# One encoder block on one core: the low-rank gate product one unit sooner, both gate transposes ahead of one half unit, and one 7-product unit fewer in the mixer's output product

## The chip, the cores and the metric

The kernel runs on one core of one Trainium2 chip. Five engines work side by side, each with its own queue of instructions: PE multiplies matrices into PSUM, DVE and ACT do elementwise work, POOL a little of it, SP issues DMAs. The metric is the device time of one run in microseconds (us), the median of the runs shown.

## The reference

All data is float32; 256 frames of width 2048. One layer does, in this order: half a SwiGLU, the mixer, cross-attention to 256 memory tokens, half a SwiGLU. The change lies in the mixer, the third line on:

```python
def reference(x, mem, ...):
    x = x + 0.5 * swiglu(rms_norm(x, ffn1_norm[l]), ...)
    h = rms_norm(x, mix_norm[l])
    proj = h @ w_in[l]
    u, q, k, v, g, a_lr = jnp.split(proj, list(IN_SPLITS), axis=-1)     # a_lr: 16 columns
    y_pool = pool_mixer(u, pool_w[l], pool_scale[l])
    y_gla = gla_mixer(q, k, v, g, a_lr, gla_w_a2[l], gla_b_a[l], gla_head_norm[l])
    x = x + jnp.concatenate([y_pool, y_gla], axis=-1) @ w_out[l]
    x = x + mem_cross_attention(rms_norm(x, xattn_norm[l]), rms_norm(mem, mem_norm[l]), ...)
    x = x + 0.5 * swiglu(rms_norm(x, ffn2_norm[l]), ...)
    return rms_norm(x, final_norm)

def gla_mixer(q, k, v, g, a_lr, w_a2, b_a, head_norm):
    log_a = jax.nn.log_sigmoid((a_lr @ w_a2 + b_a)) / GLA_GATE_TEMP     # decay of every channel
    ...  # cumulative decays within chunks of 64 frames scale q and k; chunk-causal attention -> o
    o = o * lax.rsqrt(jnp.mean(o * o, axis=-1, keepdims=True) + RMS_EPS)
    return (o * head_norm) * jax.nn.silu(g)
```

## The kernel before, in words

**Numbers.** A float32 operand is split in two parts of type fp32r: a high part (ACT's cast, `wh` for weights) and a low part (DVE's difference, `wl`). A product is three matmuls: high by high, high by low, low by high. A matmul has a moving side of 128x512.

**Units.** All weights come through one stream of units of 1 MB: 256 rows of the weight by 1024 columns. Three loads are ahead (tile `raw`, three buffers), two splits are ahead (`wh`, `wl`, three buffers). A *plain* unit (`unit_p`, its matmuls recorded at L362) takes 24 matmuls. A *7-product* unit (`unit_s` and `seven`, recorded at L507) saves one product in eight and takes 21, but needs sums: of the activations, made once by `Sums.make` (DVE at L424 to L436, ACT and DVE at L285 and L286), and of the weights, made by `split_seven` for each unit (tile `T`: DVE at L486; then ACT at L279 and L489, DVE at L280 (`xl`) and L453).

**Blocks.** `block_s` takes eight units (2048 rows) for 1024 output columns. Its `order` says in which order the eight row pairs are taken, its `sevens` which of them are 7-product units, `amid` what else is put between two of them. The plain sums live in two PSUM tiles, the extra products of the 7-product units in two more; there are four PSUM tiles in all. `combine` (L581 to L586) and `join` (L596) merge them. `behind={n: (j, f)}` makes the matmuls of half `j` of the block's n-th unit stand behind the instruction that `f` gives, in PE's queue.

**The mixer.** `w_in` is taken in four blocks: q and k, pooling, v, gates. After the first stands the low-rank unit: `load_a` (L1056), `split_a` (L1065 and two parts), `a_unit` (16 matmuls into `pa`, L1072), `ev_a` (the tile `aT`, L1081 to L1083). `decay_logits` (L1088, tile `pz`) multiplies it with `gla_w_a2` ahead of the second half of the pooling block's first unit; ACT works on it (L1094 to L1102) and `decay` takes it up on DVE (scans at L1107, then L1114). `ev_g` and `gate` finish the gates: PE turns them in two groups of eight transposes (`rows_turned`, tile `ph`, L789), group 1 before group 0, and DVE multiplies (L1253) and splits the result into the activations `ys` of the output product. That is `into_x` with the plan `MIXED`: two blocks of eight units of `w_out`, whose result is added to `x` (L779, L767); `fold` turns `x` (tile `px`, L800) and splits it into `xs` (L248, L240) for the cross-attention, whose queries (`w_q`) follow.

**Order.** The code emits work unit by unit (`Stream`): `st.op(f, n)` puts `f` behind the next n units. Within what the dependences and `in_turn`, `behind_weights` and `issue_after` allow, the framework's scheduler sets the order on each engine. The homes of a tile in memory are shared: `T` and some `xh` of the output product lie in the two buffers `kv`, which the two 1 MB halves of `mem` take over (L1325).

Of the kernel before, what the change touches and what calls it, by code (L numbers as in the profile page):

```python
# [20 lines left out]
NB = 512  # L21
# [78 lines left out]
def build(ctx, tc, I, out):  # L100
    nc = tc.nc
    st = Stream()
# [87 lines left out]
    xs = main.tile([P, KT, 2, S], F32R, tag="xs", name="xs")  # L190
# [74 lines left out]
    def behind_weights(f):  # L265

        with tc.issue_after(latest["vector"].ins), tc.issue_after(latest["scalar"].ins):
            return f()
# [366 lines left out]
    def wload(dst, w, k0, n, n0, cols=NB):  # L635
        nc.sync.dma_start(
            dst, w[k0 * P : (k0 + n) * P, n0 : n0 + cols].rearrange("(k p) n -> p k n", p=P)
        )
# [9 lines left out]
    def wwide(w, n0, k0=0, nk=KT):  # L648

        def src(k):  # L650
            def load(raw):
                raw = raw.rearrange("p (k n) -> p k n", n=2 * NB)
                if len(loaded) < 3:
                    for kk in range(2):
                        parts = (0, NB) if not loaded else (0,)
                        for c in parts:
                            n = 2 * NB // len(parts)
                            wload(raw[:, kk : kk + 1, c : c + n], w, k + kk, 1, n0 + c, n)
                else:
                    wload(raw, w, k, 2, n0, 2 * NB)  # L660
                next(first_loads, None)
                loaded.append(1)
            return load
        return [src(k0 + k) for k in range(0, nk, 2)]
# [146 lines left out]
    class IntoX:  # L811
# [7 lines left out]
        def make_sums(self, after=None):  # L819
            for g, n in zip(self.sums.pairs, after or self.after):  # L820
# [1 line left out]

    WHOLE = IntoX((0, 4), (2, 5), ((1, 2, 3, 5, 0, 6, 4, 7), (1, 2, 0, 3, 4, 5, 6, 7)),
                  ((0, 4), (0, 4)))
    MIXED = IntoX((0, 4, 6), (1, 4, 9), ((1, 2, 3, 6, 0, 5, 4, 7), (1, 2, 0, 3, 4, 5, 6, 7)),
                  ((0, 4), (0, 4, 6)), room=3, folds=(1, 1, 2, 2))
    OUTPUT = IntoX((0, 4, 6), (0, 4, 9), ((1, 2, 3, 5, 0, 6, 4, 7), (1, 2, 0, 3, 4, 5, 6, 7)),
                   ((0, 4), (0, 4, 6)), room=3, folds=(1, 1, 2, 2))
    REST = IntoX((0,), (2,), ((1, 2, 3, 4, 0, 5), None), ((0,), ()), False)
# [2 lines left out]
    def into_x(w, act, scale, gain=None, k0=0, nk=KT, spread_too=True, src=None, way=OUTPUT,  # L832
               spread_at=3, behind=None):

        for b in range(2):
            st.op(lambda b=b: fetch_x(b, src), 2)
            cols = wwide(w, b * 2 * NB, k0, nk)
            if way.sevens[b]:
                block_s(cols, act, way.sums, way.orders[b], residual(scale, b, 0),
                        early_parts(scale, b), way.sevens[b], behind=None if b else behind)  # L840
            else:
                block_t(cols, act, residual(scale, b))
            if gain is not None:
                for j in range(2):
                    st.op(lambda c=2 * b + j: fold(c, gain), way.folds[2 * b + j])
        if gain is not None:
            st.op(lambda: finish_norm(4, spread_too), way.folds[3] + 1)
            if spread_too:
                st.op(spread_norm, spread_at)
# [94 lines left out]
    def in_ys(i):  # L944
        t = ys[:, 2 * i : 2 * i + 2].rearrange("p k a s -> p (k a s)")
        return t.rearrange("p (a n s) -> p a n s", a=2, n=4)

    qk_sums = Sums("qe", xs, (1, 3), False, 2, {0: in_ys(6), 1: in_ys(7)})
# [16 lines left out]
    w_in = I["w_in"][0]  # L965
    mix = {}
# [172 lines left out]
    def turn_qk(j):  # L1139
        if "kq" not in mix:  # L1140
            mt("kq", [P, 4 * LINES])
        t = mix["k" if j else "q"] = mix["kq"][:, j * H * S : (j + 1) * H * S].rearrange(
            "p (h s) -> p h s", h=H
        )
        nc.scalar.copy(t, rows_turned(mix["rows", j]))
# [29 lines left out]
    def queries(h):  # L1175
        q, E, F = mix["q"][:, h, :], mix["E"], mix["F"]
        e = lambda c: E[:, 4 * h + c : 4 * h + c + 1]
        f = lambda i: F[:, i, h : h + 1]
        QD = mix["QD", h] = m4()
        at = QD_AT  # L1180
        factors = {(0, 1): e(1), (0, 2): f(0), (0, 3): f(2), (1, 2): e(2), (1, 3): f(1), (2, 3): e(3)}
        for j in range(3):
            nc.scalar.copy(QD[:, at[j] + j * CH : at[j] + (j + 1) * CH], q[:, j * CH : (j + 1) * CH])
            for c in range(j + 1, 4):
                nc.vector.tensor_scalar_mul(
                    QD[:, at[j] + c * CH : at[j] + (c + 1) * CH], q[:, c * CH : (c + 1) * CH],
                    factors[j, c],
                )

    def scores(h):  # L1190
        q, kd, QD, at = mix["q"][:, h, :], mix["k"][:, h, :], mix["QD", h], QD_AT
        ps = ptile(uid("pq"))
        for j in range(4):
            part = slice((j % 2) * CH, (j % 2 + 1) * CH)
            rhs = QD[:, at[j] + j * CH : at[j] + S] if j < 3 else q[:, 3 * CH :]
            nc.tensor.matmul(
                ps[part, j // 2, j * CH : S], kd[:, j * CH : (j + 1) * CH], rhs, start=True, stop=True
            )
        s = score_tile(h)
        for j in range(4):  # L1200
            part = slice((j % 2) * CH, (j % 2 + 1) * CH)
            nc.scalar.copy(s[part, j // 2, j * CH :], ps[part, j // 2, j * CH : S])
# [56 lines left out]

    ORDER_IN = (0, 2, 4, 1, 5, 3, 6, 7)  # L1260
    st.op(query_rows, 3)
    block_s(wwide(w_in, 2 * NB), xs, qk_sums, ORDER_IN, ev_qk, home=wide_home)
    st.op(lambda: turn_qk(1), 1)
    st.op(lambda: turn_qk(0), 2)
    st.unit(load_a, a_unit, split_a)
    st.op(ev_a)
    st.op(decay, 2)
    def head(h):
        attend(h)
# [2 lines left out]
    def scores_of(*hs):  # L1272
        for h in hs:
            st.op(lambda h=h: scores(h))

    def queries_of(*hs):
        for h in hs:
            st.op(lambda h=h: behind_weights(lambda: queries(h)))

    block_s(wwide(w_in, 0), xs, qk_sums, ORDER_IN, ev_pool, home=wide_home,  # L1280
            behind={0: (0, decay_logits)}, amid={4: lambda: queries_of(0, 1), 6: lambda: scores_of(0, 1)})
    for f, h, after in (
        (queries, 2, 1), (scores, 2, 1), (queries, 3, 1), (scores, 3, 1), (lambda _: turn_pool(), None, 2),
        (means, 1, 3), (means, 2, 4), (means, 3, 7), (means, 0, 8),
# [23 lines left out]
    def homes(of):  # L1308
        return lambda: scope.update(shared={tag: list(of[tag]) for tag in of})
# [27 lines left out]
    def mem_fold(c):  # L1337

        v = four(ptile(uid("tm")))
        for j in range(4):  # L1340
# [6 lines left out]

    MIXED.make_sums()
    into_x(I["w_out"][0], ys, 1.0, G_X, spread_too=False, way=MIXED,
           behind={2: (1, lambda: mix["turned", 1])})  # L1350
    st.op(homes(Q_HOMES))
    st.op(mem_in, 2)
    for c in range(4):
# [337 lines left out]
def program(shapes):  # L1691
    import concourse.bacc as _bacc

    nc = _bacc.Bacc("TRN2", target_bir_lowering=False, num_devices=1)
    args = {
        name: nc.dram_tensor(f"in_{name}", shapes[name], F32, kind="ExternalInput").ap()
        for name in _INS
    }
    out = nc.dram_tensor("out", _OUT, F32, kind="ExternalOutput").ap()
    with tile.TileContext(nc, schedule_with_timeline_sim=True) as tc, ExitStack() as ctx:  # L1700
        build(ctx, tc, args, out)
    return nc
# [10 lines left out]
```

## Time and profile before

| | |
|---|---|
| median of 3 runs (lowest, highest) | 2077.58 us (2077.37, 2078.93) |
| the profiled execution: its time, its span | 2078.92 us, 2077.1 us |
| granted PE clock | 0.999 |
| PE busy (share of the span), matmuls | 2061.7 us (99%), 9461 |
| weight loads of PE, DVE, ACT, POOL busy | 83%, 89%, 56%, 5% |

The profiled execution is 1.34 us above the median. A row of a timeline reads: start in us, length in us, engine, line, operation, out<-in, sizes, count; a bracket gives the idle time before it and what ended it. Rows of one kind that follow each other are merged. Matmuls overlap, so what counts is from start to start.

### The profile page before, as it was taken

To read this page: it belongs to the slowest core of one execution; us is meant where nothing else is said; L and a number is where in the kernel's file an instruction comes from. 1 tells how busy PE (TensorE), PEld (TensorE's weight loads), DVE (VectorE), ACT (ScalarE), POOL (GpSimd) and SP (SyncE) were. 2 spreads that over 40 slices of the span, in tenths; PEclk is the share of its full clock that TensorE was granted. 3 is DMA by queue.
4 is the path that set the end of the run, shared out by engine and by line. 5 is a ranking of instruction groups with operands and counts; after the bars stand their busy time and mean duration, and the time that the engine had idled before them with its cause. 6 is when DMAs were issued, how large, how long until landed. Compare 5 with 4: busy or idle time off the path is not lost.

```text
span 2077.1 us, 24042 instructions
## 1 busy us (share of the span) xinstructions
PE 2061.7 (99%) x9461; PEld 1713.8 (83%) x9461; DVE 1838.8 (89%) x1717; ACT 1171.3 (56%) x1190; POOL 107.5 (5%) x95
## 2 busy tenths in 40 slices
PE   9999999999999999999999999999999999999998
PEld 7888888888888887887888888888888888888886
DVE  6998899989998769889889878889988999889987
ACT  7665455554554656566755554556554555545554
POOL 0000000000000000000000000000000010000001
PEclk9999999999999999999999999999999999999999
DMA  7666766566666655457755455666576765776664
GB/s 264 203 202 223 243 210 217 184 229 235 226 198 222 234 175 183 164 197 227 266 183 196 166 183 182 203 213 216 178 243 213 236 210 192 224 241 223 207 226 155
DMA packets 122985, 435.92 MB, mean 210 GB/s; under 512 B 9844, under 2 KB 13528, under 8 KB 122488
## 3 DMA queue, kind: packets, MB, share of 16 engines
q1 hardware_dynamic: 122696, 433.86, 62.4%
q8 instruction: 74, 1.21, 0.2%
q10 hardware_dynamic: 176, 0.53, 0.1%
q14 instruction: 39, 0.32, 0.0%
HBM read 417.58 MB, written 16.78 MB: 209 GB/s over the span
## 4 chain that ended last, share of the span: by engine, by line
PE 97%; DVE 1%; ACT 1%; DMA 0%; issue 0%; SPq 0%; DVEq 0%; ACTq 0%
PE pt L362 63%; PE pt L507 29%; PE ph L789 1%; PE pl L1396 1%; PE pv L1433 1%; DVE wl L453 1%; PE px L800 0%; DMA x<-in_x 0%; PE pp L1044 0%; PE pe L362 0%; DVE T L486 0%; ACT wh L489 0%; PE pa L1072 0%; PE tm L1342 0%; PE po L1209 0%
## 5 line engine op out<-in xcount | busy, mean ns | idle before, releaser
L362 PE MATMUL pt<-wh,xs 128*128 128x512 f32 x2464 | 790.2, 391 | 0.2 <-ACT wh L279 0.2
L1671 ACT CAST wh<-raw 128x2048 fp32r<-128x2048 f32 x243 | 463.8, 1913 | 224.7 <-PE pt L362 123.7
L453 DVE TENSOR_TENSOR wl<-raw,wh 128x2048 fp32r<-128x2048 f32 (+1 forms) x243 | 516.6, 2134 | 83.1 <-ACT wh L1671 82.8
L362 PEld LDWEIGHTS pt<-wh,xs 128*128 128x128 f32 x2464 | 461.8, 188 | 95.8 <-ACT wh L279 0.6
L489 ACT CAST wh<-T 128x1024 fp32r<-128x1024 f32 x262 | 274.8, 1053 | 380.4 <-DVE T L486 367.5
L362 PE MATMUL pt<-wl,xs 128*128 128x512 f32 x1232 | 480.8, 391 | 0.7 <-DVE wl L453 0.7
L362 PE MATMUL pt<-wh,ys 128*128 128x512 f32 x1440 | 455.3, 389 | 0.0
L362 PEld LDWEIGHTS pt<-wh,ys 128*128 128x128 f32 x1440 | 270.2, 188 | 55.7
L453 DVE TENSOR_TENSOR wl<-T,wh 128x2048 fp32r<-128x2048 f32 (+1 forms) x131 | 294.4, 2247 | 8.0 <-ACT wh L489 7.6
L362 PE MATMUL pt<-wl,ys 128*128 128x512 f32 x720 | 280.9, 390 | 2.1 <-DVE wl L453 2.1
L362 PEld LDWEIGHTS pt<-wl,xs 128*128 128x128 f32 x1232 | 231.4, 188 | 48.2 <-DVE wl L453 1.1
L280 DVE TENSOR_TENSOR xl<-raw,xh 128x1536 fp32r<-128x1536 f32 x131 | 229.4, 1751 | 19.5 <-ACT xh L279 19.4
L279 ACT CAST xh<-raw 128x1536 fp32r<-128x1536 f32 x131 | 193.9, 1480 | 67.3 <-PE pt L507 43.1
L486 DVE TENSOR_TENSOR T<-T,raw 128x512 f32<-128x512 f32 x262 | 180.8, 690 | 6.7
L457 POOL TENSOR_TENSOR wl<-raw,wh 128x768 fp32r<-128x768 f32 x46 | 85.7, 1863 | 1469.4 <-DVE wl L453 1446.6
L362 PEld LDWEIGHTS pt<-wl,ys 128*128 128x128 f32 x720 | 135.2, 188 | 30.4 <-DVE wl L453 2.6
L486 DVE TENSOR_TENSOR T<-raw 128x1024 f32<-128x1024 f32 x131 | 159.5, 1218 | 0.5
L507 PE MATMUL pt<-wh,xs 128*128 128x512 f32 x392 | 152.3, 389 | 0.0
L507 PE MATMUL pt<-xh,xs 128*128 128x512 f32 x408 | 151.9, 389 | 0.0
L507 PE MATMUL pt<-wh,xe 128*128 128x512 f32 x320 | 124.3, 389 | 0.0
L507 PEld LDWEIGHTS pt<-xh,xs 128*128 128x128 f32 x408 | 76.6, 188 | 15.9
L507 PEld LDWEIGHTS pt<-wh,xs 128*128 128x128 f32 x392 | 73.6, 188 | 15.2
(270 smaller groups left out, 2073.2 us busy)
## 6 DMA issues: line engine op xcount, KB each, us to landing
raw<-in_ffn_w_down SPq DMA_DIRECT2D x88, 1024.0 KB, 5.6
raw<-in_ffn_w_up SPq DMA_DIRECT2D x80, 1024.0 KB, 5.1
raw<-in_ffn_w_gate SPq DMA_DIRECT2D x77, 1024.0 KB, 5.1
raw<-in_w_in SPq DMA_DIRECT2D x32, 1024.0 KB, 5.1
raw<-in_xattn_w_kv SPq DMA_DIRECT2D x32, 1024.0 KB, 5.0
raw<-in_w_out SPq DMA_DIRECT2D x16, 1024.0 KB, 5.9
raw<-in_xattn_w_q SPq DMA_DIRECT2D x16, 1024.0 KB, 5.7
raw<-in_xattn_w_o SPq DMA_DIRECT2D x16, 1024.0 KB, 5.7
```

What stands on the lines that cost most here:

```text
L279: in_turn("scalar", lambda: nc.scalar.copy(hi, src))
L280: in_turn("vector", lambda: nc.vector.tensor_tensor(out=lo, in0=src, in1=f32(hi), op=ALU.subtract))
L362: nc.tensor.matmul(ps, a, w, start=first and i == 0, stop=last and i == 2)
L453: in_turn("vector", lambda: nc.vector.tensor_tensor(out=lo[:, :n], in0=src[:, :n], in1=f32(hi[:, :n]), op=ALU.subtract))
L457: rest = nc.gpsimd.tensor_tensor(out=lo[:, n:], in0=src[:, n:], in1=f32(hi[:, n:]), op=ALU.subtract)
L486: in_turn("vector", lambda: nc.vector.tensor_tensor(out=o, in0=a, in1=b, op=ALU.add))
L489: in_turn("scalar", lambda: nc.scalar.copy(th[:, c], t[:, c]))
L507: nc.tensor.matmul(banks[n], x, w, start=n in fresh and j == 0, stop=n in ends and j == 2)
L789: rows["turned"] = nc.tensor.transpose(v[:, i, h * P : (h + 1) * P], g[:, h, i * P : (i + 1) * P], ident)
L1396: nc.tensor.matmul(ps[:, t, :M], ys[:, 4 * h + d, a, tok], xa["K", h][:, d, b, :], start=i == 0, stop=i == 11,)
L1433: nc.tensor.matmul(ps[:, d, :S], xa["V", h][:, m, a, col], xa["PT", h][:, m, b, :], start=i == 0, stop=i == 5,)
L1671: in_turn("scalar", lambda: nc.scalar.copy(hi, raw))
```

## The change

Three edits. The low-rank unit and its `ev_a` move from behind the first block to between its seventh and eighth unit. The output product's first block waits in its third unit for the first transposes of group 0 of the gates, not for those of group 1 (`mix["turned", b]` is the last transpose of group b; group 0 is turned after group 1). And in the second block of the output product pair 6 becomes a plain unit: its sums are no longer made, three plain units stand ahead of the first 7-product unit instead of two, and the two that are left (pairs 0 and 4) follow each other.

```diff
-    MIXED = IntoX((0, 4, 6), (1, 4, 9), ((1, 2, 3, 6, 0, 5, 4, 7), (1, 2, 0, 3, 4, 5, 6, 7)),
-                  ((0, 4), (0, 4, 6)), room=3, folds=(1, 1, 2, 2))
+    MIXED = IntoX((0, 4), (1, 4), ((1, 2, 3, 6, 0, 5, 4, 7), (1, 2, 3, 0, 4, 5, 6, 7)),
+                  ((0, 4), (0, 4)), room=2, folds=(1, 1, 2, 2))
...
-    block_s(wwide(w_in, 2 * NB), xs, qk_sums, ORDER_IN, ev_qk, home=wide_home)
+    def low_rank():
+        st.unit(load_a, a_unit, split_a)
+        st.op(ev_a)
+
+    block_s(wwide(w_in, 2 * NB), xs, qk_sums, ORDER_IN, ev_qk, home=wide_home, amid={6: low_rank})
     st.op(lambda: turn_qk(1), 1)
     st.op(lambda: turn_qk(0), 2)
-    st.unit(load_a, a_unit, split_a)
-    st.op(ev_a)
     st.op(decay, 2)
...
     into_x(I["w_out"][0], ys, 1.0, G_X, spread_too=False, way=MIXED,
-           behind={2: (1, lambda: mix["turned", 1])})
+           behind={2: (1, lambda: mix["turned", 0])})
```

What stands in the engines' queues at three places, before and now. First DVE, at the end of the first `w_in` block; `rows` L582 to L596 are the merging of that block, `wl` the low parts of weights, `wh<-ident` the clearing of the low-rank weight. Before:

```order
L1065 TENSOR_SCALAR wh_5380<-ident 128x2048
L582 TENSOR_TENSOR rows_5375<-pt_5294,rows_5375 128x512
L286 TENSOR_TENSOR wh_5380<-raw_5292,wh_5380 128x16x16
L583 TENSOR_TENSOR rows_5375<-pt_5295,rows_5375 128x1024
L586 TENSOR_TENSOR rows_5375<-pt_5295,rows_5375 128x512
L313 COPY R_5413<-ps_5410 128x256
L453 TENSOR_TENSOR wl_5416<-raw_5321,wh_5415 128x1280
L596 TENSOR_TENSOR rows_5375<-pt_5116,rows_5375 128x1024
L596 TENSOR_TENSOR rows_5375<-pt_5117,rows_5375 128x1024
L453 TENSOR_TENSOR wl_5453<-raw_5352,wh_5452 128x2048
L1082 TENSOR_TENSOR aT_5487<-pa_5458,c_5486 32x256
L1083 TENSOR_TENSOR aT_5487<-aT_5487,R_5413 32x256
```

Now:

```order
L1065 TENSOR_SCALAR wh_5347<-ident 128x2048
L286 TENSOR_TENSOR wh_5347<-raw_5251,wh_5347 128x16x16
L582 TENSOR_TENSOR rows_5374<-pt_5294,rows_5374 128x512
L583 TENSOR_TENSOR rows_5374<-pt_5295,rows_5374 128x1024
L586 TENSOR_TENSOR rows_5374<-pt_5295,rows_5374 128x512
L453 TENSOR_TENSOR wl_5380<-raw_5292,wh_5379 128x2048
L313 COPY R_5412<-ps_5409 128x256
L453 TENSOR_TENSOR wl_5415<-raw_5321,wh_5414 128x2048
L1082 TENSOR_TENSOR aT_5438<-pa_5420,c_5437 32x256
L1083 TENSOR_TENSOR aT_5438<-aT_5438,R_5412 32x256
L453 TENSOR_TENSOR wl_5443<-raw_5351,wh_5442 128x1280
```

The low-rank weight is prepared whole before the merging, and `aT` stands ahead of both `join`s. In PE's queue `pa` now stands two matmuls into the block's last unit, not behind it.

Second PE, in the first block of the output product, from the first group of transposes on (`ph`). Before:

```order
L789 MATMUL ph_6648<-ident,rows_6447 128x128 x8
L362 MATMUL pt_6622<-wh_6616,ys 128x512
L362 MATMUL pt_6622<-wl_6617,ys 128x512
L362 MATMUL pt_6622<-wh_6616,ys 128x512 x2
L362 MATMUL pt_6622<-wl_6617,ys 128x512
L362 MATMUL pt_6622<-wh_6616,ys 128x512 x2
L362 MATMUL pt_6622<-wl_6617,ys 128x512
L362 MATMUL pt_6622<-wh_6616,ys 128x512 x2
L789 MATMUL ph_6667<-ident,rows_6447 128x128
```

Now:

```order
L362 MATMUL pt_6622<-wh_6609,ys 128x512 x2
L362 MATMUL pt_6622<-wl_6610,ys 128x512
L362 MATMUL pt_6622<-wh_6609,ys 128x512
L789 MATMUL ph_6647<-ident,rows_6446 128x128 x8
L789 MATMUL ph_6666<-ident,rows_6446 128x128 x8
```

Both groups stand together now; seven of the second group's eight stood 16 matmuls later.

Third DVE, in the second block of the output product. `T` of the first 7-product unit (pair 0), the additions into `x`, then the low part `wl<-raw` of the unit that is third (now) or fourth (before) in the block. Before:

```order
L767 SCALAR_TENSOR_TENSOR x_6731<-pt_6622,x_6731 128x2x512
L486 TENSOR_TENSOR T_6949<-T_6949,raw_6855 128x512
L280 TENSOR_TENSOR xl_6953<-raw_6855,xh_6952 128x1536
L767 SCALAR_TENSOR_TENSOR x_6731<-pt_6623,x_6731 128x2x512
L453 TENSOR_TENSOR wl_6951<-T_6949,wh_6950 128x2048
L424 TENSOR_TENSOR j_6990<-ys 128x512
L431 TENSOR_TENSOR j_6990<-j_6990 128x128
L432 TENSOR_TENSOR j_6990<-j_6990 128x128
L433 SCALAR_TENSOR_TENSOR j_6990<-j_6990 128x128
L436 TENSOR_TENSOR j_6990<-j_6990 128x128
L453 TENSOR_TENSOR wl_7043<-raw_6885,wh_7042 128x2048
```

Now:

```order
L453 TENSOR_TENSOR wl_6949<-raw_6854,wh_6948 128x2048
L486 TENSOR_TENSOR T_7022<-raw_6884 128x1024
L767 SCALAR_TENSOR_TENSOR x_6730<-pt_6621,x_6730 128x2x512
L767 SCALAR_TENSOR_TENSOR x_6730<-pt_6622,x_6730 128x2x512
L486 TENSOR_TENSOR T_7022<-T_7022,raw_6884 128x512 x2
L280 TENSOR_TENSOR xl_7026<-raw_6884,xh_7025 128x1536
L453 TENSOR_TENSOR wl_7024<-T_7022,wh_7023 128x2048
L486 TENSOR_TENSOR T_7064<-raw_6918 128x1024
```

The sums of pair 6 are gone and pair 3's low part stands ahead of pair 0's work. On SP the two loads of `mem` now stand one ahead of and one behind the load of the last unit of `w_out`; before they stood behind the second load of `w_q`.

More of the change, by code (lines that the diff above doesn't have):

```diff
@@ L1280, in build @@
     block_s(wwide(w_in, 0), xs, qk_sums, ORDER_IN, ev_pool, home=wide_home,
-            behind={0: (0, decay_logits)}, amid={4: lambda: queries_of(0, 1), 6: lambda: scores_of(0, 1)})
+            behind={0: (0, decay_logits)},
+            amid={4: lambda: queries_of(0, 1), 6: lambda: scores_of(0, 1)})
     for f, h, after in (
```

## The prediction

> **What bounds the kernel now.** The page first: the span and the busy shares.
>
> ```profile
> span 2077.1 us, 24042 instructions
> PE 2061.7 (99%) x9461; PEld 1713.8 (83%) x9461; DVE 1838.8 (89%) x1717; ACT 1171.3 (56%) x1190; POOL 107.5 (5%) x95
> ```
>
> PE is idle for 15.4 us of the span; any edit can win only there, or by giving PE less to do. The view of waits, for PE alone, names the causes (total, times, longest):
>
> ```profile
> PE pt L362 <- DVE wl L453: 2.8, 2, 2.1
> PE pt L507 <- DVE xl L280: 0.7, 2, 0.5
> ```
>
> So within the matmul stream PE waits four times, always for DVE. PE's timeline gives the places. Two rows first for the rate (24 matmuls from 956.90 to 962.34), then each wait with the matmul ahead of it and one far enough behind.
>
> ```profile
> 956.90 0.39 PE L362 MATMUL pt<-wh,ys 128*128 128x512 f32 x1
> 962.34 0.39 PE L507 MATMUL pt<-xh,ye 128*128 128x512 f32 x1
> ...
> 781.46 0.61 PE L362 MATMUL pt<-wh,xs 128*128 128x512 f32 x2
> 782.77 0.50 PE L362 MATMUL pt<-wl,xs 128*128 128x512 f32 x1 [0.70 <-DVE wl L453]
> 787.91 0.62 PE L507 MATMUL pt<-xh,xs 128*128 128x512 f32 x2
> ...
> 940.67 0.39 PE L507 MATMUL pt<-wh,ye 128*128 128x512 f32 x1
> 941.59 0.50 PE L507 MATMUL pt<-xl,ys 128*128 128x512 f32 x1 [0.53 <-DVE xl L280]
> ...
> 966.15 0.39 PE L362 MATMUL pt<-wh,ys 128*128 128x512 f32 x1
> 968.67 0.50 PE L362 MATMUL pt<-wl,ys 128*128 128x512 f32 x1 [2.14 <-DVE wl L453]
> 973.79 0.39 PE L507 MATMUL pt<-xh,ys 128*128 128x512 f32 x1
> ...
> 1065.70 0.50 PE L507 MATMUL pt<-xl,xs 128*128 128x512 f32 x1 [0.19 <-DVE xl L280]
> ```
>
> A matmul costs 5.44 / 24 = 0.2267 us from start to start. A wait costs more than its bracket, since the length of a matmul (0.39) reaches past the next start, and PE restarts slowly. I take the stretch less its matmuls: **A**, pooling block: 781.46 to 787.91, 24 matmuls, 6.45 - 5.44 = 1.01. **B**, first output block: 940.67 to 956.90, 67 matmuls, 16.23 - 15.19 = 1.04. **C**, second output block: 966.15 to 973.79, 23 matmuls, 7.64 - 5.21 = 2.43. Together 4.48 us. The fourth, at 1065, lies past the output product.
>
> In C's stretch the view by windows (PE, PEld, DVE, ACT, POOL; clock; DMA share) shows DVE full:
>
> ```profile
> 950.00:1000.00 50.00, 47.86 (x220) 39.56 (x219) 49.06 (x48) 26.76 (x33) 0.00 (x0) 1.00 0.79 270
> ```
>
> The granted clock is 1.00, so nothing here is a throttled PE.
>
> **The change: one plain unit for a 7-product unit.** This adds 24 - 21 = 3 matmuls: 3 x 0.2267 = 0.68 us, all on PE's path. [...] The rows above give 226.7 ns, so I keep 0.68.
>
> On DVE it takes away pair 6's sums and that unit's `T` and `xl`. Its own rows from C's place:
>
> ```profile
> 962.23 2.28 DVE L453 TENSOR_TENSOR wl<-T,wh 128x2048 fp32r<-128x2048 f32 x1
> 964.43 0.68 DVE L424 TENSOR_TENSOR j<-ys 128x512 f32<-128x512 f32 x1
> ...
> 966.13 0.29 DVE L436 TENSOR_TENSOR j<-j 128x128 f32<-128x128 f32 x1
> 966.34 2.28 DVE L453 TENSOR_TENSOR wl<-raw,wh 128x2048 fp32r<-128x2048 f32 x1
> 968.54 1.22 DVE L486 TENSOR_TENSOR T<-raw 128x1024 f32<-128x1024 f32 x1
> ...
> 971.05 2.04 DVE L240 SCALAR_TENSOR_TENSOR xs<-px,gains,xs 128x256 fp32r<-128x256 f32 x5
> ...
> 973.48 1.41 DVE L486 TENSOR_TENSOR T<-T,raw 128x512 f32<-128x512 f32 x2
> ```
>
> The sums last from 964.43 to 966.34, 1.91; a `T` 1.22 + 1.41; an `xl` 1.75 (row 939.78 below). Some 6.3 us of DVE work go from a stretch where DVE has 0.94 us of slack in 50.
>
> More than that, the low part for which C waits (966.34) now stands ahead of all of pair 0's work. It passes, by these lengths, `T` 2.63, `xl` 1.75, the low part of `T` 2.28, the sums 1.91 and the two additions into `x`, for which I take the 1.22 that DVE needs for the 1024 columns of `T`: 11.0 us. So it starts near 955.3 and ends near 957.6. PE comes to it after two plain units: they begin at 951.2 (956.90 less 25 matmuls) and last 10.9, so at 962.1, or 961.1 once B's 1.04 are gone. C goes, with 3.5 us of lead, 5 if B's shift of 1.5 (below) reaches DVE here.
>
> What is late next: pair 4's unit now follows pair 0's at once. With the shift the third unit's low part ends near 956.1; pair 0's `T`, `xl`, low part and the additions take 9.1, to 965.2. PE gets to pair 0 at 961.1 + 5.4 + two groups of eight transposes (1.6 to 2.1 by the `ph` row below), 968.3. From there DVE has pair 4's `T` 2.63, eight L240 at 2.04 / 5 = 0.41, and `xl` 1.75, 7.6 in all: 972.8, and 975.1 with the low part. PE needs that `xl` after 25 matmuls (5.7), at 974.0, and the low part two us later. The lead is about 1 us: enough, but the thinnest spot of the change. What may come back here is bounded by 0 and C's own 2.43.
>
> **The gates' turning.** One order edit, no work added.
>
> ```profile
> 917.09 1.03 PE L789 MATMUL ph<-ident,rows 128*128 128x128 f32 x8
> 921.76 0.93 PE L789 MATMUL ph<-ident,rows 128*128 128x128 f32 x7
> 922.73 1.66 DVE L1253 SCALAR_TENSOR_TENSOR t<-m,gains,ph 128x256 f32<-128x256 f32 x4 [1.50 <-PE ph L789]
> 939.78 1.75 DVE L280 TENSOR_TENSOR xl<-raw,xh 128x1536 fp32r<-128x1536 f32 x1
> 941.45 2.28 DVE L453 TENSOR_TENSOR wl<-T,wh 128x2048 fp32r<-128x2048 f32 x1
> ```
>
> DVE was free for group 0 at 922.73 - 1.50 = 921.23; the transposes, now right behind group 1's, end near 919. The 1.50 go, and what follows on DVE up to 941.5 is a chain without idle time on DVE (the chain of waits runs through it), so `xl` is done near 939.95. Without the wait PE would ask for it at 940.67 + 0.23 = 940.90: lead 0.95. The low part behind it ends near 942.2 and is asked for nine matmuls later, 942.9: lead 0.7. B's 1.04 go. What stands behind the transposes on PE is delayed by less than 1 us against its old place and loses nothing in total. Were the cover gone (a shift below 0.55), up to 1.04 stay.
>
> **The low-rank unit.** The same instructions, earlier.
>
> ```profile
> 741.84 1.50 DVE L1065 TENSOR_SCALAR wh<-ident 128x2048 fp32r<-128x2048 f32 x1 [1.51 <-PE pt L507]
> ...
> 752.75 3.79 PE L1072 MATMUL pa<-xs,wh 128*128 128x512 f32 x16
> 762.84 1.99 PE L1088 MATMUL pz<-aT,wa 32*128 32x256 f32 x8
> 754.81 1.33 ACT L1134 ACTIVATE rows<-rows,Rq 128x512 f32<-128x512 f32 x2
> 774.46 1.06 ACT L1102 ACTIVATE m<-m 128x1024 f32<-128x1024 f32 x1
> 775.55 1.23 DVE L1103 SCALAR_TENSOR_TENSOR m<-m,m 128x1024 f32<-128x1024 f32 x1 [3.30 <-ACT m L1102]
> 779.29 1.23 DVE L1114 TENSOR_TENSOR m<-m 128x1024 f32<-128x1024 f32 x1
> 780.43 2.28 DVE L453 TENSOR_TENSOR wl<-raw,wh 128x2048 fp32r<-128x2048 f32 x1
> ```
>
> A's low part (780.43) stands behind the decay, which waits for ACT, which waits for `pz`. `pa` moves 22 matmuls up, to 752.75 - 4.99 = 747.76; its 16 matmuls and the 34 that now follow put `pz` at 759.1, 3.7 sooner. The weight for it is cleared on DVE in the first gap that used to be idle (1.51 ahead of 741.84), so it is ready long before. Its load on SP is one place up, in front of a 1 MB load that had 4 us in hand. ACT gives something back: the scalings L1134 (twice 1.33) now stand ahead of the work on `pz`, and I take off 1 us. DVE's scans then start 2.7 sooner, the low part ends near 780.0, and PE asks at 781.91: lead 1.9. A's 1.01 go; the bounds are 0 and 1.01 won.
>
> **Sum.** -1.01 - 1.04 - 2.43 + 0.68 = -3.80 us. Against the profiled execution: 2078.92 - 3.80 = 2075.12. It lies 1.34 above the median; from the median, 2077.58 - 3.80 = 2073.8. That is 0.18%, and about 0.2% (4.15 us, to 2073.4) is what a measurement of this kernel can tell from no change.
>
> **Rivals.** *The wait at 1065 goes too* (chance 0.17). A, B and C cost 0.3 to 0.5 more than their brackets; with its bracket of 0.19 this one costs about 0.6, and the time would be 2073.2. For it: DVE enters the cross-attention with less behind it. Against it:
>
> ```profile
> 1062.37 1.48 ACT L279 CAST xh<-raw 128x1536 fp32r<-128x1536 f32 x1 [11.44 <-PE pt L507]
> ```
>
> ACT waits there 11.44 us for PE itself to free the buffer, so the wait moves with PE.
>
> *A wait comes back at pair 4's unit, or B goes only in part* (0.13): half of C or B, 1.0 to 2.4 returned, 2074.8 to 2076.2. It decides where DVE loses over 1 us of its lead.
>
> *Nothing is won* (0.07): DVE stays the bound of the stretch, the waits change their places, and PE has its three matmuls more: 2078.3. [...]
>
> *Slower through SP's queue* (0.13). The loads of `mem` move up between those of `w_out` and `w_q`, and the first waits until PE has read pair 0's `xh`, some 18 matmuls into that unit, near 972.5. What such a pair did before, and the page's row for one load (median us to landing at the end):
>
> ```profile
> 987.77 1.97 SPq L1325 DMA_DIRECT2D mem<-in_mem  x2
> 1000.08 1.92 ACT L1671 CAST wh<-raw 128x2048 fp32r<-128x2048 f32 x1 [6.26 <-DMA raw<-in_xattn_w_q]
> ...
> raw<-in_xattn_w_q SPq DMA_DIRECT2D x16, 1024.0 KB, 5.7
> ```
>
> From 972.5 on `mem`, `w_out`, `mem`, `w_q` have to land in this order. PE needs `w_q`'s first unit when it is through pairs 0 and 4 (42 matmuls, 977.8) and three plain units (16.3): at 994.1, less 1.92 for the cast and 2.28 for the low part, so 4.35 us for each megabyte. Before, the three megabytes from 987.77 to 1000.08 came at 4.1 each, which is just enough. Landing one after the other at 5.7 each they are 5.4 us late, and the seven units behind lose 5.7 - 5.44 each, 1.8: 2073.8 + 7.2 = 2081.0, worse with what `x` stores beside it. It decides at 4.35 us. Against it: the window row has the DMA engines at 0.79, and a median landing overlaps its neighbours.
>
> **How the numbers follow.** The sum as it stands has 0.50. It ends 0.4 above the bound of 0.2%, and the terms are good to half a microsecond or so, so I give nine twentieths of it to "faster", 0.23, and three quarters of the first rival, 0.13. Of the last rival's 0.13, 0.08 lies past the bound on the other side. The rest, 0.56, is within 0.2%. The range leaves out the last rival's worse part and the ends of the others: 2072.3 to 2078.5, with "nothing is won" inside.
>
> **What would show it.** In the new profile: no bracket on PE between 700 and 1010; `pz` near 759; no idle time on DVE ahead of the second L1253 group; three matmuls more. Wrong would be: a bracket for `xl` or `wl` at pair 4's unit of the second block; a cast that waits for `w_out` or `w_q` past 980 with PE idle behind it; brackets as before at 782, 941 or 968.

## The result, and the profile after

| | median (lowest, highest) | runs |
|---|---|---|
| before | 2078.49 us (2077.37, 2079.35) | 14 |
| after | 2073.65 us (2073.18, 2075.22) | 14 |
| ratio | 0.9977, 95% interval 0.9970 to 0.9984 | |

The change makes the kernel 0.23% faster. The forecast was 2073.8. The page of the profile after, its first lines, and the view of waits for PE alone, whole run:

```profile
span 2071.8 us, 24035 instructions
PE 2060.3 (99%) x9464; PEld 1714.2 (83%) x9464; DVE 1833.3 (88%) x1706; ACT 1168.7 (56%) x1186; POOL 105.9 (5%) x94
PE pwarm L206 <- POOL ident masks.py:199: 1.4, 1, 1.4
PE px L726 <- DMA x<-in_x: 0.7, 1, 0.7
PE pt L362 <- ACT xs L236: 0.5, 1, 0.5
PE pt L507 <- DVE xl L280: 0.2, 1, 0.2
```

PE has three matmuls more. The 2.8 for `wl` are gone and of the 0.7 for `xl` 0.2 is left: A, B and C are no more. That 0.2 is the wait at 1065, which the first rival would have taken away. The other waits shown, the 0.5 for `xs` too (at 5.92), stand in the first 10 us. DVE's window in C's stretch, to set against the 49.06 of before:

```profile
950.00:1000.00 50.00, 50.00 (x230) 41.66 (x229) 44.04 (x44) 29.88 (x40) 0.00 (x0) 1.00 0.81 285
```

PE is busy for all of it, DVE for 5.0 us less.

To compare kernels without the noise of the start I use PE's timeline at four points that all of them have: the 16 transposes ahead of the mixer (L800), the first matmul of the mixer's linear attention (L1209), the last 16 transposes of the output product (L800), and the last matmul of the program. Of the kernel after, these rows:

```profile
681.41 1.91 PE L800 MATMUL px<-ident,x 128*128 128x128 f32 x16
859.20 0.60 PE L1209 MATMUL po<-ST,rows 128*128 128x256 f32 x2
1002.55 1.91 PE L800 MATMUL px<-ident,x 128*128 128x128 f32 x16
2062.83 0.39 PE L362 MATMUL pt<-wh,ys 128*128 128x512 f32 x1
```

The three stretches hold edit 1 (place A), edits 2 and 3 (B and C), and nothing that was edited. All profiles of this study, in us:

| kernel | first | second | third | sum |
|---|---|---|---|---|
| before, first profile | 178.83 | 146.20 | 1060.28 | 1385.31 |
| before, three more | 178.83, 178.82, 178.82 | 145.92, 145.73, 147.79 | 1060.29, 1060.24, 1060.29 | 1385.04, 1384.79, 1386.90 |
| after, twice | 177.79, 177.79 | 143.35, 143.36 | 1060.28, 1060.31 | 1381.42, 1381.46 |
| low-rank unit alone | 177.79 | 148.08 | 1060.26 | 1386.13 |
| gates' turning alone | 178.83 | 144.93 | 1059.79 | 1383.55 |
| plain unit alone | 178.84 | 144.46 | 1060.24 | 1383.54 |
| three 7-product units | 177.79 | 144.42 | 1060.27 | 1382.48 |
| the same, pair 5 sooner | 177.79 | 142.91 | 1060.06 | 1380.76 |
| relief only | 177.79 | 143.36 | 1060.27 | 1381.42 |
| pair 6's first sum twice | 178.85 | 147.07 | 1060.27 | 1386.19 |

The third stretch holds 4890 matmuls, but 4889 in the run with pair 5 sooner and 4888 in that of the turning alone: there the transposes stand one or two matmuls later (0.23 each) and the second stretch has them. The sum is free of that.

Against the first profile of before the change wins 3.89 us here, where the sum said 3.80. The spans differ by 5.3: the other 1.4 lie ahead of 682, nearly all of it in the first 10 us, where PE waits for the loads of `x` (its second group of transposes of `x` starts at 9.98 before, at 8.66 after) and which no edit touches.

### The profile page after: what moved, and what is told of

Read it like the earlier page. It is cut to its first block, busy times and chain, and to the rows that moved or that the text cites. A ratio compares the mean times of both kernels' runs of the same rounds, so it can differ in the third digit from the quotient of the medians.

```text
span 2071.8 us, 24035 instructions
## 1 busy us (share of the span) xinstructions
PE 2060.3 (99%) x9464; PEld 1714.2 (83%) x9464; DVE 1833.3 (88%) x1706; ACT 1168.7 (56%) x1186; POOL 105.9 (5%) x94
## 4 chain that ended last, share of the span: by engine, by line
PE 99%; DMA 0%; DVE 0%; ACT 0%; SPq 0%; issue 0%; DVEq 0%; ACTq 0%
PE pt L362 64%; PE pt L507 30%; PE ph L789 2%; PE pl L1399 1%; PE pv L1436 1%; PE px L800 1%; PE pp L1044 0%; PE pe L362 0%; DMA x<-in_x 0%; PE pa L1072 0%; PE tm L1345 0%; PE po L1209 0%; PE px L726 0%; PE pq L1196 0%; DVE wl L453 0%
```

## Experiments: the edits one at a time

The low-rank unit alone:

```diff
-    block_s(wwide(w_in, 2 * NB), xs, qk_sums, ORDER_IN, ev_qk, home=wide_home)
...
+    block_s(wwide(w_in, 2 * NB), xs, qk_sums, ORDER_IN, ev_qk, home=wide_home, amid={6: low_rank})
...
-    st.unit(load_a, a_unit, split_a)
-    st.op(ev_a)
```

> Only the low-rank unit is moved; the turning and the second half of the output product stay as before. Main theory (the time is TensorE's stream, and each edit takes away its own wait): the wait for the low part in the pooling block, near 782, is gone, the ones near 941 and 968 stay at about 0.53 and 2.14, and from the transposes ahead of the mixer (L800 on px) to the end the kernel is 1.0 us shorter: 2077.5, ratio 0.9995. Rival (the waits are coupled, VectorE's lateness is handed on from block to block): the wait near 941 changes too, by over 0.2. Second rival (the start belongs to the changed program): the first L726 transposes wait 0.7 for x in this kernel as in the full change and not 1.5.

Measured: 2077.27 us (2076.26 to 2079.02, 11 runs), before on the same chip 2078.18 (33 runs), ratio 0.9995 (0.9986 to 1.0003). The first stretch is 1.04 shorter, as A's price said, the wait near 941 stays at 0.49, and PE's first wait for `x` is 0.30, not 0.7: neither rival holds. But the second stretch is 1.9 longer than in the first profile of before. C's wait is 2.63, longer by 0.5, and that is not all. PE's timeline there:

```profile
964.02 0.39 PE L362 MATMUL pt<-wh,ys 128*128 128x512 f32 x1
967.04 0.80 PE L362 MATMUL pt<-wl,ys 128*128 128x512 f32 x1 [2.63 <-DVE wl L453]
967.63 1.05 PE L362 MATMUL pt<-wh,ys 128*128 128x512 f32 x2
968.48 0.63 PE L362 MATMUL pt<-wl,ys 128*128 128x512 f32 x1
```

The view by windows of the same place (length; PE, PEld, DVE, ACT, POOL; granted clock; DMA share; GB/s):

```profile
964.40:966.40 2.00, 0.01 (x1) 0.00 (x0) 1.97 (x3) 1.88 (x6) 0.00 (x0) 1.00 0.96 387
966.40:966.80 0.40, 0.00 (x0) 0.00 (x0) 0.40 (x1) 0.00 (x0) 0.00 (x0) 0.83 1.08 440
966.80:969.80 3.00, 2.76 (x7) 2.19 (x8) 3.00 (x7) 1.05 (x1) 0.00 (x0) 0.50 0.78 197
969.80:970.20 0.40, 0.40 (x3) 0.35 (x2) 0.40 (x3) 0.00 (x0) 0.00 (x0) 0.65 0.95 389
```

Behind the wait two matmuls take 0.85 us from start to start where 0.45 is usual. The clock falls to half at 966.66 (0.83 over the 0.4 us from 966.40) and is back at 970.08, 3.42 us later. So this wait cost a third item beside its bracket and its restart: matmuls at half speed. Neither the main theory nor its rivals had that. Six of the 11 runs have a mean clock of 0.998 and a median of 2078.6, the other five 0.999 and 2077.2.

The gates' turning alone (the diff's `mix["turned", 1]` to `mix["turned", 0]`):

> Only the gates' turning is moved. Main theory: the wait for xl near 941 is gone, the one near 782 stays at 0.70. The earlier VectorE reaches the second output block too: by the 1.5 us that VectorE gains less the 1.0 that TensorE gains, the wait of 2.14 near 968 shrinks by about 0.5. Together 1.0 to 1.5 us: 2077.0 to 2077.5. Rival (the wait near 968 moves with TensorE): it grows to about 3.2, since TensorE comes 1.0 earlier to a low part that ends when it did, and nothing is won: 2078.5.

Measured: 2076.25 us (2075.21 to 2077.70, 11 runs), ratio 0.9989 (0.9980 to 0.9998). No bracket near 941, 0.70 still at 782, and C's is 1.50 instead of 2.14. The main theory holds: what DVE gains beyond PE, 0.5, is handed on to C. The bracket alone does not show that, since it differs from run to run in the kernel before; the section on the clock takes that part off. The median falls by 1.9, more than the 1.0 to 1.5 forecast; three of these 11 runs have the lower mean clock, against 16 of the 33 of before.

The output product's second block alone (the line of `MIXED`):

> Only the second half of the output product is changed (three plain units first, two 7-product units). Main theory: the wait near 968 is gone (2.43 with its restart), three matmuls more cost 0.68, the waits near 782 and 941 stay: 1.75 us shorter, 2076.75. VectorE's lead at pair 4's unit is smaller by 0.5 than in the full change (about 0.5 left), and by the rival a bracket of up to 1 us for xl or wl shows at pair 4's unit: 2077.7.

Measured: 2076.32 us (2075.17 to 2076.70, 11 runs), ratio 0.9990 (0.9981 to 0.9999); the sum of stretches falls by 1.77 against 1.75 expected. C is gone, 0.70 and 0.50 stay at 782 and 941, and nothing comes back at pair 4's unit.

## Experiments: what takes C away

The kernel after, but with three 7-product units in the new order; and, in the second run, pair 5 ahead of pair 4 as well (the last line is the second run's):

```diff
-    MIXED = IntoX((0, 4), (1, 4), ((1, 2, 3, 6, 0, 5, 4, 7), (1, 2, 3, 0, 4, 5, 6, 7)),
-                  ((0, 4), (0, 4)), room=2, folds=(1, 1, 2, 2))
+    MIXED = IntoX((0, 4, 6), (1, 4, 9), ((1, 2, 3, 6, 0, 5, 4, 7), (1, 2, 3, 0, 4, 5, 6, 7)),
+                  ((0, 4), (0, 4, 6)), room=3, folds=(1, 1, 2, 2))
...
+    MIXED = IntoX((0, 4, 6), (1, 4, 9), ((1, 2, 3, 6, 0, 5, 4, 7), (1, 2, 3, 0, 5, 4, 6, 7)),
```

> The full change, but the second half of the output product keeps three 7-product units (pairs 0, 4, 6 with their sums) in the new order, three plain units first. It tells the order of the units from VectorE's relief. If the order alone took away the wait near 968: no bracket there or behind it, three matmuls fewer than the full change, 0.68 us under it: 2073.0. If VectorE's relief was needed: pair 6's sums, T and xl put back some 6.3 us on VectorE ahead of pair 6's unit, and TensorE waits there, by 1 to 3 us: 2074 to 2076.

Measured: 2074.60 us (2074.09 to 2076.28, 11 runs), ratio 0.9982 (0.9973 to 0.9990). C's wait is gone, and two small ones stand around the start of pair 4's unit, not at pair 6's as was expected:

```profile
971.06 0.47 PE L507 MATMUL pt<-wh,ys 128*128 128x512 f32 x1 [0.31 <-DVE xs L240]
973.24 0.50 PE L507 MATMUL pt<-xl,ys 128*128 128x512 f32 x1 [0.32 <-DVE xl L280]
```

The second stretch is 1.06 longer than after's although PE has three matmuls fewer there (0.68): 1.74 are lost, at these two waits, at a stop of 0.36 without a bracket just ahead (968.39), and in the slow restarts (the first two matmuls behind each wait are 0.31 and 0.34 apart, where 0.23 is usual). So the order alone takes C's wait away, but of C's 2.43 us 1.74 come back here: pair 6's sums make DVE late at the next unit that needs it.

> The full change with three 7-product units kept, and one more plain unit ahead of pair 4's (order 1, 2, 3, 0, 5, 4, 6, 7). In the run with three 7-product units TensorE waited twice for VectorE at pair 4's unit, 0.31 and 0.32, and lost some 1.4 us there with the restarts. One plain unit more ahead of it gives VectorE 5.4 us and asks 2.3 of it (the low part of pair 5): both waits go, pair 6's unit comes 1.4 earlier to an xl that was 1.9 ahead there. So no bracket in the second output block, three matmuls fewer than the full change: 0.68 us under it, 2073.0 where the full change has 2073.65, and the best of all. Rival (VectorE has no time left in this block, the wait only moves): a bracket of 0.3 to 1 at pair 6's unit, 2073.7 to 2074.5.

Measured: 2073.22 us (2072.68 to 2074.12, 9 runs), ratio 0.9976 (0.9966 to 0.9985); the kernel after, on the same chip, 2074.24. No bracket in the second output block; PE's waits in the whole run, but for the first, are

```profile
PE px L726 <- DMA x<-in_x: 0.6, 1, 0.6
PE pt L507 <- DVE xl L280: 0.2, 1, 0.2
```

and by windows

```profile
950.00:1000.00 50.00, 50.00 (x230) 41.66 (x229) 48.84 (x47) 28.59 (x40) 0.00 (x0) 1.00 0.80 280
```

DVE works 48.84 of these 50 us, as before the change (49.06), and PE waits for nothing: the sum of stretches is 0.68 under that of after, the three matmuls. This beats both kernels, the one after by 1.0 us of the medians (0.4 to 1.4, by resampling the 9 and 11 runs). The plain unit that the change pays for was not needed; one plain unit more ahead of pair 4's does the same.

The relief without the order (pair 6 plain, the old order 1, 2, 0, 3, 4, 5, 6, 7):

> The full change, but the second output block keeps the old order (two plain units ahead of pair 0's), with pair 6 plain. It tells VectorE's relief (no sums of pair 6, 1.91 us ahead of the low part that C waits for) from the order. By the sum: 2.14 less 1.91 less the 0.5 that the turning hands on leaves no wait, lead 0.3, and the time is that of the full change, 2073.65. If the order is what matters: a bracket of 0.5 to 2 near 967, 2074.5 to 2076.5.

Measured: 2073.87 us (2073.41 to 2075.56, 11 runs), ratio 0.9978 (0.9969 to 0.9987), stretches as after's to 0.01. The low part that C waited for, and the matmul that reads it:

```profile
960.83 2.29 DVE L453 TENSOR_TENSOR wl<-raw,wh 128x2048 fp32r<-128x2048 f32 x1
963.45 0.39 PE L362 MATMUL pt<-wl,ys 128*128 128x512 f32 x1
```

It ends at 963.12, 0.33 ahead; 0.3 was worked out. So either half of edit 3, the order or the relief, takes C's wait away; the relief, with the two other edits, is enough by itself. The lead is thin: in this profile DVE had waited 0.82 us near 946 for a load of weights, in the first profile of after 1.14.

## Experiments: the clock behind C's wait, and the start

The kernel after once more, beside the run with pair 5 sooner:

> The full change again, beside the run above on one chip. If the start belongs to the program, TensorE's first wait for x is 0.7 again; if it is chance, it lies anywhere between 0.3 and 1.6, as in the five other profiles. Its times should have a narrower spread than those of the kernel before, and hardly a run with the lower mean clock, since no wait of 2 us is left after which the clock could fall: 2073.7, within 1 us.

Measured: 2074.24 us (2073.47 to 2074.97, 11 runs), before 2078.57 (31 runs), ratio 0.9979 (0.9971 to 0.9988). The first wait for `x` is 1.48 in this profile, 0.72 in the first one of the same kernel: chance, not the program. Over all profiles it lies between 0.30 and 2.11. The 11 runs lie within 1.5 us, the 31 of before within 3.7, and one of the 11 has the lower mean clock, as was expected.

DVE's first addition for pair 6 done twice in the kernel before:

```diff
+            for _ in range(2 if self is twice.get("sums") and g == 6 else 1):
+                nc.vector.tensor_tensor(
+                    out=a.rearrange("p (k s) -> p k s", k=2), in0=f32(act[:, k, 0, :]),
...
+    twice["sums"] = MIXED.sums
```

> The kernel before, with VectorE's first addition of pair 6's sums in the second output block done twice (0.61 us more on VectorE ahead of the low part that C waits for). C's bracket becomes about 2.75. Theory of the clock (after about 2.2 us of idle TensorE its granted clock falls to 0.50 for 3.4 us, as the low-rank run showed behind a wait of 2.63): in more than half of the runs the matmuls behind the wait go at half speed, and the time is 0.6 + 1.4 = 2.0 us above the faster runs of the kernel before (2077.5): 2079.5, with a mean clock of 0.998. Rival (the clock has no part): every run 0.6 us more, 2078.8 by the median, no more runs with the lower clock than before.

Measured: 2078.90 us (2078.16 to 2079.89, 11 runs), ratio 1.0 (0.9992 to 1.0009). The test missed its aim: the scheduler put matmuls of a 7-product unit ahead of the plain unit that reads the low part, and the one wait became two, 1.65 for DVE's work on `xs` and 0.68 for `wl` (2.33 in all, with matmuls between them). All 11 runs have a mean clock of 0.999. That fits the rival for the time (2078.8), but says nothing on a wait of 2.75 in one piece, which it did not make.

So the kernel before itself, unchanged, three more times:

> The kernel before, unchanged, profiled anew. Theory of the clock: C's wait, 2.14 in the profile shown, lies at the edge of what makes TensorE's granted clock fall, so in about half of its executions (mean clock 0.998 where the others have 0.999) the clock is 0.50 for 3.4 us behind C's wait, the matmuls there are 0.43 us apart, and 1.4 us more are lost. In such a profile the window from 968 to 971 shows a clock near 0.50, and the stretch from the L800 transposes at 682 to the end is 1386.7 and not 1385.3. Rival (the lower mean clock comes from somewhere else, the start or the tail): the clock behind C's wait is 1.00 in every profile.

> As the run above: the kernel before once more, since about half of the executions should show it. A mean clock of 0.998 goes with a clock of 0.50 for 3.4 us behind C's wait and with a stretch of 1386.7; a mean clock of 0.999 goes with 1.00 there and with 1385.3.

> As the two runs above, once more. Besides, the first wait for x at the start should differ from run to run between 0.3 and 1.6, and move everything behind it by as much.

Measured: 2078.67, 2077.34 and 2079.61 us, mean clocks 0.999, 0.999 and 0.998. C's wait is 1.88, 1.68 and 2.19: it differs from run to run. What differs is a load of weights. In the profile of before that the prediction reads, ACT waits for it, and DVE for ACT:

```profile
947.80 1.92 ACT L1671 CAST wh<-raw 128x2048 fp32r<-128x2048 f32 x1 [1.73 <-DMA raw<-in_w_out]
949.75 2.29 DVE L453 TENSOR_TENSOR wl<-raw,wh 128x2048 fp32r<-128x2048 f32 x1 [1.01 <-ACT wh L1671]
```

The same two rows in the second of the three runs:

```profile
946.11 1.91 ACT L1671 CAST wh<-raw 128x2048 fp32r<-128x2048 f32 x1 [1.24 <-DMA raw<-in_w_out]
948.06 2.29 DVE L453 TENSOR_TENSOR wl<-raw,wh 128x2048 fp32r<-128x2048 f32 x1 [0.52 <-ACT wh L1671]
```

From here to the low part that C waits for, DVE's timeline has no bracket, so what is lost here should be lost at C as well. The six profiles that have both waits in one piece bear it out:

| kernel | DVE's wait for these weights | C's wait | difference |
|---|---|---|---|
| before, four profiles | 1.01, 0.72, 0.52, 0.99 | 2.14, 1.88, 1.68, 2.19 | 1.13, 1.16, 1.16, 1.20 |
| low-rank unit alone | 1.47 | 2.63 | 1.16 |
| gates' turning alone | 0.86 | 1.50 | 0.64 |

So a third to a half of C's wait in the kernel before comes from this load, and the 0.5 by which it was longer in the run of the low-rank unit is the load's too. What the turning hands on is 1.16 less 0.64, 0.52: 0.5 was expected. That an earlier load would take 0.5 to 1 us off C with no edit to the units follows from the table, but no run tests it.

The third run has the half clock; PE's timeline in it,

```profile
967.80 0.50 PE L362 MATMUL pt<-wl,ys 128*128 128x512 f32 x1 [2.19 <-DVE wl L453]
968.14 0.62 PE L362 MATMUL pt<-wh,ys 128*128 128x512 f32 x2
968.60 0.59 PE L362 MATMUL pt<-wl,ys 128*128 128x512 f32 x1
968.99 1.05 PE L362 MATMUL pt<-wh,ys 128*128 128x512 f32 x2
```

and its windows:

```profile
967.80:968.40 0.60, 0.60 (x3) 0.51 (x4) 0.60 (x1) 0.00 (x0) 0.00 (x0) 1.00 0.67 273
968.40:968.80 0.40, 0.40 (x3) 0.36 (x2) 0.40 (x2) 0.00 (x0) 0.00 (x0) 0.78 0.03 10
968.80:971.80 3.00, 3.00 (x8) 2.32 (x8) 3.00 (x10) 1.05 (x1) 0.00 (x0) 0.50 0.85 262
971.80:972.20 0.40, 0.40 (x2) 0.30 (x2) 0.40 (x3) 0.00 (x0) 0.00 (x0) 0.70 0.92 379
```

The clock falls at 968.62, 0.8 us after PE had begun again, and is back at 972.04. The second stretch is 147.79: 1.6 more than with a wait of 2.14 and a full clock (146.20). The expected sums were 1386.7 with the half clock and 1385.3 without; measured are 1386.90, and 1385.04 and 1384.79. This is the kernel before, so the half clock is shown in it and not only in a relative.

How often? The 64 runs of before in the two timed comparisons: 26 with a mean clock of 0.999, median 2077.7; 38 below it (16 of 33 in one, 22 of 31 in the other), of which 35 with 0.998, median 2079.1. The kernels whose output product has no long wait (after in both its sets, pair 5 sooner, relief only, three 7-product units) have 0.998 in 8 of 56 runs, and these are no longer than the others; a mean to three digits also takes in the clock's fall at the program's end (0.82 from 2060 to 2077 in the first profile of before), so it counts the case only roughly. Three runs of before with 0.997 (2081.7 to 2082.0) stay unexplained.

The half clock lasts 3.42 us both times. In the run of the low-rank unit it begins inside the wait, 2.25 us after PE had fallen idle (964.41 to 966.66); in the run of before it begins after a whole wait of 2.19, when work had resumed. Behind the 2.14 of the first profile of before the clock is 1.00 (968.60 to 972.00). Two cases, and 0.05 us between a wait that has the half clock behind it and one that has not, do not show what sets it off.

## Why the prediction was right, point by point

- **A, -1.01.** Measured -1.04, in each of the profiles that have the edit. `pa` stands at 747.76 and `pz` at 759.2 on the clock of before (746.40 and 757.83, plus the 1.36 by which the start differs): 747.76 and 759.1 were worked out. The low part now ends at 778.73 and is asked for at 780.29: lead 1.56, not 1.9. By itself the edit shows its worth only like for like: its profile has the half clock behind C's wait, and its sum, 1386.13, is 0.8 above the first of before but 0.8 below the one of before that has the half clock too (1386.90).
- **B, -1.04.** The wait is gone with edit 2 alone. Of DVE's 1.5 us ahead of the second L1253 group none is left. The sum of the stretches falls by 1.76: B, and the 0.64 by which C's bracket is shorter there (0.5 handed on, 0.15 from the load).
- **C, -2.43, with +0.68.** -1.77 in the sum by edit 3 alone, -1.75 expected, against the first profile of before. Edits 2 and 3 together: 143.35 against 146.20, -2.85, where the sum has -2.79; against the two other profiles with a full clock, 145.92 and 145.73, it is -2.57 and -2.38.
- **Thinnest spot.** Pair 4's `xl` and low part:

```profile
969.27 1.75 DVE L280 TENSOR_TENSOR xl<-raw,xh 128x1536 fp32r<-128x1536 f32 x1
970.94 2.28 DVE L453 TENSOR_TENSOR wl<-T,wh 128x2048 fp32r<-128x2048 f32 x1
971.50 0.39 PE L507 MATMUL pt<-xl,ys 128*128 128x512 f32 x1
973.53 0.39 PE L507 MATMUL pt<-wl,ys 128*128 128x512 f32 x1
```

  The leads are 0.48 and 0.31, where about 1 was forecast: the place was right, the margins a half and a third as wide. The run with three 7-product units showed what stands behind it.
- **SP's queue.** `mem` is issued at 969.20, and ACT waits for weights as feared, but PE does not:

```profile
984.55 1.92 ACT L1674 CAST wh<-raw 128x2048 fp32r<-128x2048 f32 x1 [3.17 <-DMA raw<-in_xattn_w_q]
987.76 4.49 DVE L453 TENSOR_TENSOR wl<-raw,wh 128x2048 fp32r<-128x2048 f32 x2
991.89 0.39 PE L362 MATMUL pt<-wl,xs 128*128 128x512 f32 x1
```

  The first low part of `w_q` ends near 990, 1.9 ahead of the matmul that reads it. The loads overlapped, as the prediction held against this rival: the four megabytes issued from 969.20 to 975.45 (`mem`, `w_out`, `mem`, `w_q`) had landed when ACT starts on the first of `w_q` at 984.55, 15.35 us after the first issue, 3.84 each, where the rival took 5.7.
- **Where it was off.** The likeliest case was put within 0.2% (2073.8 and 0.18%), and the measurement says 0.23%. The step that was mis-sized is C's price, taken as one number from one execution and as DVE's work alone: the window that showed DVE full begins at 950, just behind the 1.01 us in which DVE waited for weights. The sentence "nothing here is a throttled PE" was true of that execution only. C's wait costs the stretch 2.0 to 2.4 us with a full clock (145.73 to 146.20, less 144.46 plus 0.68: 1.95 to 2.42) and 4.0 with the half clock (147.79), and the half clock came in one of four profiles of before and, as far as the mean clocks tell, in about half of its runs. The median of three, 2077.58, lies in the cheaper group; that of 14 is 2078.49. The change takes both away. The nearness of the forecast to 2073.65 owes something to this: from 2078.49 the sum of 3.80 would have given 2074.7. In the stretches the change wins 3.89, 3.62, 3.37 and 5.48 against the four profiles of before; 3.80 lies nearest to the one from which its terms were read.
- **"Nothing is won"** did not come: 3.89 us were won in the stretches. Its premise, that DVE bounds the stretch, had the shares of before on its side: PE's 99% is made of matmuls that overlap (0.39 us long, 0.2267 from start to start), by its weight loads PE is at 83%, below DVE's 89%, and in the window from 950 to 1000 DVE is the fuller, 49.06 us against PE's 47.86.

## What to carry to other kernels

A wait on TensorE is priced from several executions, not one: this one had 1.7 to 2.2 us, and in the execution with 2.19 the clock also went to half for 3.4 us, which no bracket shows; read the granted clock in windows of half a microsecond behind each long bracket. Follow the engine that is waited for further back: here a load of weights, 17 us ahead of the wait, made 0.5 to 1 us of it in four profiles. Before paying matmuls to relieve the engine that is waited for, try its order: here one plain unit in another place gave the same as a plain unit bought for 0.68 us. Where the start is noisy (here the first wait for `x` is 0.30 to 2.11 us), compare timelines between two matmuls that both kernels have; two profiles of the kernel after agreed to 0.04 us there, while their spans were 0.6 apart.

## What the hardware showed that was not expected

- The granted clock fell to 0.50 after waits of 2.63 and 2.19 us, not after waits of 2.14, 1.88, 1.68, 1.65 and 1.50, stayed there for 3.42 us, and cost 1.4 to 1.6 us. Once it fell only 0.8 us after the matmuls had begun again.
- Loads landed at different times in the same program. PE's wait for `x` at the start is 0.72 and 1.48 us in two profiles of the kernel after and 0.79 to 2.11 in four of before (0.30 to 2.11 over all 13 profiles). A load of `w_out` near 948 kept DVE waiting 0.52 to 1.01 us in the four profiles of before, and C's wait followed it: the difference of the two is 1.13 to 1.20.
